# Seven weight tiles whose low halves are made by ScalarE and an adding transfer instead of VectorE

## The chip, the cores and the metric

The kernel runs on one core of one Trainium2 chip. A core has TensorE (matrix products), VectorE (DVE in the profile), ScalarE (ACT), GpSimd (POOL), SyncE (SP, which here only issues transfers) and 16 DMA engines that move data. The metric is the device time of one launch in microseconds, lower is better; the median of the runs is compared.

## The reference

One decoder layer on 256 tokens of width 1024, in float32. The input is normalised, multiplied by one wide weight matrix, and cut into the inputs of three token mixers, their gates and the merge logits:

```python
h = rmsnorm(x, g_in)
z = h @ w_in
(mq, mk, mv, mg, dq, dk, dv, dg, iq, ik, iw, xq, xg, glog) = jnp.split(z, offs, axis=-1)
ya = moba_attention(rope(mq), rope(mk), mv);  ya = (ya * silu(mg)) @ w_up_moba
yb = dsa_attention(rope(dq), rope(dk), dv, rope(iq), rope(ik), iw);  yb = (yb * silu(dg)) @ w_up_dsa
kv = rmsnorm(mem, g_mem) @ w_mem_kv
yc = cross_attention(xq, xk, xv);  yc = (yc * silu(xg)) @ w_up_cross
u = gates[:, :, 0] * ya + gates[:, :, 1] * yb + gates[:, :, 2] * yc
out = final_rmsnorm(x + u @ w_out)
```

With 256 tokens the first mixer is plain causal attention with 8 heads. The second lets each query see only the 64 keys with the highest score of an indexer; the kernel finds them in eight rounds of "take the eight largest". The third attends to 256 memory tokens with 4 heads.

## The kernel before

**Products in halves.** Each float32 operand is split into two numbers of TensorE's shorter float32 format (`F32R`): a high half, the operand rounded, and a low half, the operand minus its high half. Each product is then three matmuls: high by high, high by low, low by high. So each weight tile is needed three times over: as it is loaded (raw), as high half, as low half.

**Steps.** The weights are cut into tiles of 512 KB, 128 rows by 1024 columns of float32. `plan.steps` lists them in the order of use; one step is the matmuls of one tile. Steps 30 and 31 make the memory keys (first half), 32 and 33 the cross queries, 34 to 37 the values of the second mixer (`dv`), 38 and 39 the second half of the memory keys, 40 to 43 the memory values (`xv`), 44 onward the gates. Between the two halves of a step, and before it, stands other work that is due there: `at(step, fn)` puts it in `plan.side`. In the steps concerned here this is the attention of the first mixer (up to step 34), the indexer (27 to 42), the rotation of the second mixer's queries and keys (`qk_swap`, four transfers on SP each; `qk_rope` and `qk_halves`), and the first scores of the cross attention and of the second mixer from 41.5 on.

**Loads.** `load_weights(s)` (line 240) loads tile s from SP's queue into one of four raw buffers (`WRAW = 4`). It is written six steps ahead of its use, but a buffer must be free for it: all that read the old tile in it must be done.

**Splits.** `split_weights(s)` is written three steps ahead of use (`SPLIT_AHEAD = 3`). Line 253, on ScalarE, writes the high half `w..h`; line 255, on VectorE, writes the low half `w..l`:

```python
last_hi[0] = nc.scalar.copy(hi[:, ks, :], raw[:, ks, :]).ins
...
nc.vector.tensor_sub(lo[:, ks, :], raw[:, ks, :], hi[:, ks, :].bitcast(F32))
```

From step 4 on `part` is the whole tile, so there is one copy and one subtraction for each tile. High and low halves have five buffers each, so the split of tile s waits until TensorE is done with tile s - 5.

**Order.** TensorE's and GpSimd's instructions run in the order in which the program writes them (`manual_schedule`). For ScalarE, VectorE and SP a planner decides the order before the launch, from its own estimates of when each instruction could start. On each engine the instructions then run strictly one after the other, each waiting for its semaphores.

**GpSimd** has in the steps concerned only the scaling of the attention's probabilities (`self_scale`, line 622, two instructions for a head) and four small copies for the indexer (lines 445 and 446). It issues no transfer. The names in the profile: `mpr` are probabilities of the first mixer, `mtp` their transposes, `mph` and `mpl` the halves of these, `mya` and `myT` the attention's results, `msc` its scores, `mms` the masked scores, `lg` and `rl` the indexer's logits before and after the rectifier, `acc` their weighted sum, `iqt` and `ikt` transposes for the indexer, `dqT`, `dkT`, `dqsw`, `dksw` queries and keys of the second mixer and their swapped copies.

**Accumulators.** TensorE writes to eight banks: four for the steps' products, two for scores and logits (tag `sc`), one for transposes (`tp`), one for attention results (`y`). A bank that hasn't been read out holds up the next matmul that writes it.

Of the kernel before, what the change touches and what calls it, by code (L numbers as in the profile page):

```python
# [11 lines left out]
OP = mybir.AluOpType  # L12
# [69 lines left out]
LO_BEHIND = {29: "mpl0"}  # L82

MEM = (2, 7, 11, 15, 21.5)


def block_places(blocks, nk):
# [8 lines left out]
class Steps:  # L96
# [11 lines left out]
    def at(self, step, fn, *args):  # L108
        self.side[step].append((fn, args))
# [3 lines left out]
def hybrid_layer_kernel(  # L113
# [14 lines left out]
    nc = tc.nc  # L128
# [116 lines left out]
    def split_weights(s):  # L245
        raw = loaded.pop(s)
        shape = list(raw.shape)
        hi = ws.tile(shape, F32R, name=f"w{s}h", tag="whi")
        lo = ws.tile(shape, F32R, name=f"w{s}l", tag="wlo")
        part = 1 if s < HALVED + 2 else shape[1]  # L250
        for j in range(0, shape[1], part):
            ks = slice(j, j + part)
            last_hi[0] = nc.scalar.copy(hi[:, ks, :], raw[:, ks, :]).ins
            with tc.issue_after(marks[LO_BEHIND[s]]) if s in LO_BEHIND else nullcontext():
                nc.vector.tensor_sub(lo[:, ks, :], raw[:, ks, :], hi[:, ks, :].bitcast(F32))
        halves[s] = (hi, lo)
# [679 lines left out]

    for pair, s0 in enumerate(MEM[0:4]):
        at(s0, mem_load, pair)
# [4 lines left out]

    at(MEM[4], mem_stats)
    at(MEM[4] + 2, rstd_rows, m_rstd, mB, "mB")
    for hf in range(2):
# [43 lines left out]
    for s in range(-SPLIT_AHEAD, n):  # L990
        p, rest = divmod(s + SPLIT_AHEAD, 2)
        if p < 4 and not rest:
            first[p]()
        if s == 4:
            nc.sync.dma_start(cst, consts[:, 0:512])
            nc.sync.dma_start(tabT.rearrange("p t c -> p (t c)"), consts[:, 512:1024])
        for fn, args in plan.side.pop(s, []):
            fn(*args)
        if LOAD_AHEAD <= s + LOAD_AHEAD < n:
            load_weights(s + LOAD_AHEAD)  # L1000
        if s + SPLIT_AHEAD < n:
            split_weights(s + SPLIT_AHEAD)
            if s + SPLIT_AHEAD == 0:
                load_late()
        if s >= 0:
            w = halves.pop(s)
            plan.steps[s][1](w, 0)
            for fn, args in plan.side.pop(s + 0.5, []):
                fn(*args)
            plan.steps[s][1](w, 1)  # L1010
# [64 lines left out]
```

## Time and profile before

| what | before |
|---|---|
| median of 3 runs | 323.46 us (322.6 to 324.31) |
| profiled execution: span from the first to the last instruction | 321.2 us |
| median of the runs less that span | 2.3 us |
| TensorE busy | 313.0 us, 97% |
| VectorE busy | 252.1 us, 78% |
| ScalarE busy | 202.4 us, 63% |
| GpSimd busy | 42.1 us, 13% |
| transfers from GpSimd's queue | none |
| moved by all transfers | 59.45 MB, 185 GB/s on the mean |

The profile records one execution. For the profiled execution only its span is known, not a time of its own beside it; the time of a run holds also what lies before the first and after the last instruction. "Busy" is the time in which at least one instruction of an engine runs. TensorE's matmuls overlap, so gaps between them are read best from their starts. A row of the timeline has start, duration, engine, line, operation, output and inputs, and, in brackets, how long the engine had stood idle before it and who released it. A row of transfers has the queue that issued it, the count, the size, and the median time from issue to landing.

### The profile page before, as it was taken

What the parts mean: (1) busy time and instruction counts of PE and PEld (TensorE: products, weight loads), DVE (VectorE), ACT (ScalarE), POOL (GpSimd) and SP (SyncE); (2) the same over time, 40 slices, a digit from 0 to 9 for tenths busy, and PEclk for the clock granted to TensorE, in tenths of its full rate; (3) what the DMA queues carried; (4) which work ended last, traced back from release to release, by engine and by line L of the source; (5) the groups of instructions that cost most, each with busy time, mean ns of one, the idle gap of its engine ahead of it and who ended that gap; (6) DMA issues with size and microseconds to landing.
All of it is one profiled execution on the core that took longest, in us unless ns stands there. A gap on an engine that the chain in (4) does not pass through costs nothing.

```text
span 321.2 us, 6394 instructions
## 1 busy us (share of the span) xinstructions
PE 313.0 (97%) x2442; PEld 298.2 (93%) x2442; DVE 252.1 (78%) x458; ACT 202.4 (63%) x357; POOL 42.1 (13%) x58
## 2 busy tenths in 40 slices
PE   8999999999999999999999999999999999999992
PEld 7899999998999989889999999999999999998882
DVE  3579999999799999988866669999466866677533
ACT  5599665687877636477666688755454546653434
POOL 0001000017202000020200235411000111014011
PEclk9999999999999999999999999999999999999997
DMA  7999886965545346484444434488756666656003
GB/s 214 376 334 326 267 264 183 282 222 138 191 131 141 126 137 229 158 254 138 134 133 131 135 130 133 134 261 271 221 178 193 192 192 198 185 157 187 2 0 131
DMA packets 18367, 59.45 MB, mean 185 GB/s; under 512 B 2208, under 2 KB 2464, under 8 KB 18336
## 3 DMA queue, kind: packets, MB, share of 16 engines
q1 hardware_dynamic: 17760, 57.73, 57.3%
q10 hardware_dynamic: 576, 1.31, 1.1%
q8 instruction: 19, 0.31, 0.4%
q14 instruction: 12, 0.10, 0.1%
HBM read 55.89 MB, written 1.05 MB: 177 GB/s over the span
## 4 chain that ended last, share of the span: by engine, by line
PE 83%; ACT 5%; DVE 5%; DMA 3%; issue 2%; SPq 0%; ACTq 0%; DVEq 0%
DMA w3r<-w_in 2%; PE i_0ps L286 2%; PE i_1ps L286 2%; PE xv_0ps L286 2%; PE dv_0ps L286 2%; PE xv_1ps L286 2%; PE dv_1ps L286 2%; PE lg L486 1%; PE o_0ps L261 1%; PE o_0ps L262 1%; PE o_0ps L260 1%; DMA w0r<-w_in 1%; ACT mpr L612 1%; PE dya L648 1%; PE mv_1ps L286 1%
## 5 line engine op out<-in xcount | busy, mean ns | idle before, releaser
L753 POOL TENSOR_TENSOR u<-u,gt 128x512 f32<-128x512 f32 x7 | 9.9, 1413 | 76.7 <-DVE gt L750 76.7
L622 POOL TENSOR_SCALAR dpr<-dpr,dst 128x128 f32<-128x128 f32 (+1 forms) x16 | 6.6, 426 | 83.4 <-DVE dst L620 83.2
L622 POOL TENSOR_SCALAR mpr<-mpr,mst 128x128 f32<-128x128 f32 (+1 forms) x16 | 9.8, 628 | 56.0 <-DVE mst L620 56.0
L740 ACT ACTIVATE gt<-gt,x_first 128x256 f32<-128x256 f32 x24 | 10.9, 501 | 3.7 <-DVE gt L737 3.6
L612 ACT ACTIVATE dpr<-dms,dst 128x128 f32<-128x128 f32 (+1 forms) x16 | 7.1, 445 | 3.6 <-DVE dst L608 3.6
L612 ACT ACTIVATE mpr<-mms,mst 128x128 f32<-128x128 f32 (+1 forms) x16 | 7.1, 445 | 2.1 <-DVE mst L608 2.1
L794 ACT ACTIVATE junk<-xn 128x512 f32<-128x512 f32 (+1 forms) x5 | 2.7, 543 | 8.6 <-DVE xn L792 8.6
L670 ACT ACTIVATE xpr<-xsc,xst,xs_rstd 128x256 f32<-128x256 f32 x8 | 4.5, 560 | 4.1 <-DVE xst L666 4.1
L758 ACT CAST us<-u 128x512 fp32r<-128x512 f32 x4 | 2.5, 623 | 6.2 <-POOL u L753 4.9
L490 ACT ACTIVATE rl<-lg 128x384 f32<-128x384 f32 x8 | 3.9, 486 | 2.7 <-PE lg L486 1.6
L653 ACT COPY dyT<-dya 64x256 f32<-64x256 f32 x8 | 2.9, 368 | 4.2 <-PE dya L648 4.0
L493 DVE SCALAR_TENSOR_TENSOR acc<-rl,iw,acc 128x128 f32<-128x128 f32 (+1 forms) x14 | 5.4, 433 | 0.1
L974 PE MATMUL warm<-ones 128*128 128x128 f32 x18 | 4.2, 430 | 1.1 <-DVE eps_t L969 1.1
L486 PE MATMUL lg<-ikT,iqT 128*128 128x128 f32 (+1 forms) x32 | 5.1, 281 | 0.1
L608 DVE CUSTOM_DVE_ANT_0 mms<-msc,bias_c 128x128 f32<-128x128 f32 (+1 forms) x16 | 5.0, 348 | 0.0
L974 PEld LDWEIGHTS warm<-ones 128*128 128x128 f32 x18 | 3.9, 330 | 1.0 <-DVE eps_t L969 1.0
L635 DVE TENSOR_TENSOR dpl<-dtp,dph 128x384 fp32r<-128x384 f32 x8 | 4.4, 555 | 0.4
L654 DVE TENSOR_TENSOR dyT<-dyT,dya 64x256 f32<-64x256 f32 x8 | 3.3, 418 | 1.8 <-ACT dyT L653 1.7
L608 DVE CUSTOM_DVE_ANT_0 dms<-dsc,sel 128x128 f32<-128x128 f32 (+1 forms) x16 | 4.7, 353 | 0.0
L634 ACT CAST dph<-dtp 128x384 fp32r<-128x384 f32 x8 | 3.8, 479 | 1.4 <-PE dtp L633 1.3
L504 DVE MATCH_REPLACE8 wk<-m,wk 128x128 f32<-128x128 f32 (+1 forms) x14 | 4.7, 345 | 0.0
L792 DVE TENSOR_TENSOR xn<-o_0ps,xn 128x512 f32<-128x512 f32 x2 | 1.4, 692 | 4.2 <-PE o_0ps L262 4.2
(1296 smaller groups left out, 1544.3 us busy)
## 6 DMA issues: line engine op xcount, KB each, us to landing
x_rows<-x SPq DMA_DIRECT2D x2, 512.0 KB, 8.9
eT<-memT SPq DMA_DIRECT2D x4, 256.0 KB, 4.6
xn<-x SPq DMA_DIRECT2D x2, 512.0 KB, 4.8
w0r<-w_in SPq DMA_DIRECT2D x2, 256.0 KB, 3.3
w1r<-w_in SPq DMA_DIRECT2D x2, 256.0 KB, 4.3
xT<-xT SPq DMA_DIRECT2D x2, 256.0 KB, 6.6
w2r<-w_in SPq DMA_DIRECT2D x1, 512.0 KB, 6.7
w3r<-w_in ACTq DMA_DIRECT2D x1, 512.0 KB, 7.8
```

Of the source, the lines that this page charges most:

```text
L286: nc.tensor.matmul(accs[nm][t][:, :n], a[p](k, slice(t * P, (t + 1) * P)), w[q][:, half, :], start=k + i == 0, stop=k + i == nk + 1,)
L486: nc.tensor.matmul(lg[:, c : c + n], q[:, q0:q1], idx["k"][:, j, 0:n], start=j == 0, stop=j == 1)
L493: nc.vector.scalar_tensor_tensor(acc[:, c], rl[:, c], iw[:, t, g : g + 1], (bias_c if g == 0 else acc)[:, c], op0=OP.mult, op1=OP.add,)
L504: nc.vector.match_replace(out=wk[:, c], in_to_replace=m8[t], in_values=src[:, c], imm_value=TAKEN)
L608: nc.vector.tensor_tensor_reduce(out=ms[:, c], in0=sc[:, c], in1=bias()[:, c], op0=OP.add, op1=OP.min, scale=-(HD**-0.5), scalar=3e38, acc ...
L612: big["last_exp"] = nc.scalar.activation(pr[:, c], ms[:, c], AF.Exp, bias=st[:, t : t + 1], scale=-1.0, accum_out=st[:, 2 + t : 3 + t],)
L622: nc.gpsimd.tensor_scalar(pr[:, c], pr[:, c], st[:, 4 + t : 5 + t], 1.0, op0=OP.mult, op1=OP.mult)
L635: marks[f"{nm}pl{hd}"] = nc.vector.tensor_sub(pl, tp[:, 0 : 3 * P], ph.bitcast(F32)).ins
L670: big["last_exp"] = nc.scalar.activation(pr3[:, t, :], sc[:, t, :], AF.Exp, bias=st[:, t : t + 1], scale=xs_rstd[:, t : t + 1], accum_out= ...
L740: nc.scalar.activation(gt[:, f, :], gt[:, f, :], AF.Sigmoid, bias=x_first[:, j : j + 1])
L753: adder.tensor_tensor(u, u, gt, op=OP.add)
L974: nc.tensor.matmul(warm[:, 0:P], ones, ones, start=True, stop=True)
```

## The change

For seven tiles, every second one from step 31 to step 43, the low half is made in another way. ScalarE first rounds the raw tile to the high half as before. Then ScalarE multiplies the raw tile by -1 and writes it, rounded, into the low half's buffer: this is the high half negated. Then a transfer issued by GpSimd adds the raw tile to what stands in that buffer, which leaves raw minus high half. VectorE's subtraction is gone for these tiles; the other tiles are split as before.

```diff
+LO_ADDED = (31, 33, 35, 37, 39, 41, 43)
...
             last_hi[0] = nc.scalar.copy(hi[:, ks, :], raw[:, ks, :]).ins
+            if s in LO_ADDED:
+                nc.scalar.mul(lo[:, ks, :], raw[:, ks, :], -1.0)
+                nc.gpsimd.dma_start(lo[:, ks, :], raw[:, ks, :], accum_op=OP.add)
+                continue
             with tc.issue_after(marks[LO_BEHIND[s]]) if s in LO_BEHIND else nullcontext():
                 nc.vector.tensor_sub(lo[:, ks, :], raw[:, ks, :], hi[:, ks, :].bitcast(F32))
```

## The prediction

> **What bounds the kernel now.** I read the page's busy line and chain of waits first, then the table of windows, then the list of whom TensorE waited for, and last the timelines of each engine between 80 and 142 us, where tiles 31 to 43 are split.
>
> ```profile
> span 321.2 us, 6394 instructions
> PE 313.0 (97%) x2442; PEld 298.2 (93%) x2442; DVE 252.1 (78%) x458; ACT 202.4 (63%) x357; POOL 42.1 (13%) x58
> PE 83%; ACT 5%; DVE 5%; DMA 3%; issue 2%; SPq 0%; ACTq 0%; DVEq 0%
> ...
> 84.00:88.00 4.00, 3.79 (x36) 3.65 (x35) 3.94 (x7) 2.96 (x6) 0.00 (x0) 1.00 0.44 131
> 92.00:96.00 4.00, 3.88 (x36) 3.37 (x35) 3.94 (x15) 3.48 (x11) 0.00 (x0) 1.00 0.43 131
> 112.00:116.00 4.00, 4.00 (x19) 3.20 (x18) 3.94 (x13) 2.46 (x3) 0.00 (x0) 1.00 0.41 131
> ...
> 220.00:280.00 60.00, 60.00 (x517) 60.00 (x516) 40.04 (x38) 32.57 (x42) 5.17 (x4) 1.00 0.66 200
> ```
>
> TensorE is the bound: 97% busy, 83% of the chain, and the clock granted is full in these windows. After each colon pair the columns are length, then busy time of PE, PEld, DVE, ACT and POOL. VectorE (third busy figure) is nearly full from 84 to 116 us, 3.94 of 4.00, so it looks like a second bound; but a busy engine is worth something only where TensorE waits for it. In 112 to 116 us PE loses nothing, in 220 to 280 us neither. Where it does lose:
>
> ```profile
> PE iqt L459 <- DVE mst L608: 0.4, 1, 0.4
> PE ikt L463 <- DVE mpl L635: 0.2, 1, 0.2
> ...
> 79.47 0.28 PE L459 MATMUL iqt<-ident_r,iqs 128*128 128x128 f32 x1 [0.36 <-DVE mst L608]
> 85.23 0.36 PE L463 MATMUL ikt<-ident_r,iks 128*128 128x128 f32 x2 [0.21 <-DVE mpl L635]
> ...
> 92.25 0.33 PE L476 MATMUL msc<-mkhi,mqhi 64*128 64x128 f32 x2
> ...
> 92.93 0.28 PE L476 MATMUL msc<-mkhi,mqlo 64*128 64x256 f32 x2
> ...
> 94.42 0.28 PE L261 MATMUL dk1ps<-xlo,w29h 128*128 128x256 f32 x1
> 94.53 0.28 PE L262 MATMUL dk1ps<-xhi,w29l 128*128 128x256 f32 x1
> 94.93 0.73 PE L486 MATMUL lg<-ikT,iqT 128*128 128x128 f32 x4
> ```
>
> The 0.4 us wait for iqt ends at 79.47 us, before the first tile that the change touches is split (81.83, below). From tile 31 on, two places are left in the stretch of the change: 0.21 us before ikt, and 0.28 us before lg (0.40 from start to start where the matmuls before it come 0.11 to 0.12 apart). Together 0.49 us: with every removed VectorE instruction free, about 0.15% of the span is to be had there, since TensorE's order is written out and its matmuls follow each other without gaps elsewhere.
>
> **What is removed: seven subtractions on VectorE.** Line 255 takes 1.20 to 1.23 us for such a tile (two rows here), 8.5 us in all. What that is worth is read at the two places.
>
> ```profile
> 82.91 1.23 DVE L255 TENSOR_TENSOR w31l<-w31r,w31h 128x1024 fp32r<-128x1024 f32 x1 [1.41 <-ACT w31h L253]
> 84.62 0.56 DVE L635 TENSOR_TENSOR mpl<-mtp,mph 128x384 fp32r<-128x384 f32 x1
> ...
> 90.76 1.21 DVE L255 TENSOR_TENSOR w33l<-w33r,w33h 128x1024 fp32r<-128x1024 f32 x1
> ...
> 94.24 0.28 DVE L608 CUSTOM_DVE_ANT_0 mms<-msc,bias_c 128x128 f32<-128x128 f32 x1
> ```
>
> At lg: VectorE runs without a gap from w33l to mms, whose reading of the scores frees the bank that lg writes. Without w33l, mms could start once the scores are there, 92.93 + 0.28 = 93.2 us, over a microsecond earlier: the whole 0.28 us goes. At ikt: mpl follows w31l and a short addition; without w31l it is bounded by ScalarE's part, the next paragraph. The other five subtractions lie where PE loses nothing; taking them away is worth 0 there, hidden behind PE's own stream.
>
> **What is added on ScalarE: seven negations.** No row shows one with a scale of -1 on this shape; the nearest are the cast of the same tile (1.05 us) and the scaled copy below (two of 256 columns in 0.91 us, so up to 1.8 us for 1024). I take 1.05 us, the row of the same shape, 7.4 us in all.
>
> ```profile
> 81.83 1.05 ACT L253 CAST w31h<-w31r 128x1024 fp32r<-128x1024 f32 x1
> 82.90 0.36 ACT L653 COPY myT<-mya 64x256 f32<-64x256 f32 x1
> 83.29 0.48 ACT L634 CAST mph<-mtp 128x384 fp32r<-128x384 f32 x1
> ...
> 89.16 1.05 ACT L253 CAST w33h<-w33r 128x1024 fp32r<-128x1024 f32 x1 [0.76 <-PE dk1ps L261]
> 90.11 0.49 ACT L490 ACTIVATE rl<-lg 128x384 f32<-128x384 f32 x1
> 91.66 0.50 ACT L490 ACTIVATE rl<-lg 128x384 f32<-128x384 f32 x1 [1.06 <-PE lg L486]
> ...
> 108.61 1.05 ACT L253 CAST w37h<-w37r 128x1024 fp32r<-128x1024 f32 x1 [0.60 <-PE xq1ps L261]
> 120.43 1.05 ACT L253 CAST w41h<-w41r 128x1024 fp32r<-128x1024 f32 x1 [1.79 <-PE dv_1ps L286]
> ...
> 139.84 0.91 ACT L680 ACTIVATE xpr<-xpr,xst 128x256 f32<-128x256 f32 x2
> ```
>
> The scaled copy runs between exponentials with no table load, so I count none. Put right behind its cast, the negation of 31 holds back myT and mph by about 1.0 us: mph ends at 84.8 instead of 83.8, mpl can start there instead of at 84.62, and ikt is 0.2 us later than now. So this place gains nothing and loses 0.2. The negation of 33 falls into the gap of 1.06 us between the two rl; the first rl ends at 91.7 instead of 90.6, and the scores at 92.25 us that need its bank don't wait. From 108 us on ScalarE waits before almost every cast. Worth of both engines' edits together: 0.28 saved, 0.2 lost, about 0.1 us gained; the bounds are 0.49 gained and, without the gaps as cover, three negations before 104 us on the path, 3 x 1.05 = 3.2 us lost.
>
> **What is added on POOL: seven transfers.** They are issued from GpSimd's queue, in program order: 31 behind the scaling of head 5, 33 between head 6 and head 7, the rest behind head 7. Behind 33 waits only head 7's scaling, wanted by the transposes two steps later; behind 43 the next attention's scaling. The raw tile now stays occupied until its transfer has landed, and with it the load four tiles on, and everything behind that load on SP. Let X be the time from issue to landing. No transfer from GpSimd, and none that adds, is in this trace.
>
> ```profile
> q1 hardware_dynamic: 17760, 57.73, 57.3%
> x_rows<-x SPq DMA_DIRECT2D x2, 512.0 KB, 8.9
> w37r<-w_in SPq DMA_DIRECT2D x1, 512.0 KB, 3.7
> w41r<-w_kv SPq DMA_DIRECT2D x1, 512.0 KB, 3.5
> ...
> 96.81 1.82 POOL L622 TENSOR_SCALAR mpr<-mpr,mst 128x128 f32<-128x128 f32 x4 [14.64 <-DVE mst L620]
> 91.99 0.33 SPq L240 DMA_DIRECT2D w37r<-w_in  x1
> 97.31 1.15 SPq L530 DMA_DIRECT2D dksw<-dkT  x2
> 121.92 1.22 DVE L537 TENSOR_TENSOR dksw<-dksw,tabT 128x1024 f32<-128x1024 f32 x1
> ...
> 120.65 0.40 PE L286 MATMUL dv_0ps<-w37l,xhi 128*128 128x512 f32 x1
> 131.85 0.40 PE L286 MATMUL xv_0ps<-w41l,ehi 128*128 128x512 f32 x1
> ```
>
> A plain load of 512 KB lands in 3.5 to 3.7 us in this stretch. The addition reads its destination too; one tile's bytes cost 0.573 x 321.2 us x 0.524 MB / 57.73 MB = 1.7 us of all sixteen engines. For the issue on GpSimd I add 1 us, an estimate between the issue on SP (0.33) and the 1.82 us in which POOL does four instructions. X is then about 3.6 + 1.7 + 1 = 6.3 us; its bounds are a plain load, 3.5, and the slowest landing of this size, 8.9.
>
> The Trainium skill, "DMA: Bandwidth & Descriptors" (Anatomy of one DMA), fits a GpSimd transfer as 2.0 us plus its bytes at 436 GB/s, 3.2 us here. "Collectives: The Full Stack" (The bandwidth ceiling) says an addition in the DMA engine is slower because it reads two sources, not because it adds; with the bytes counted twice an estimate from the fit is 4.4 us. No row shows either; by them the margin worked out next would be wider and the sum the same.
>
> Which X hurts? The addition of 33 can't be issued before head 6 is scaled, 96.81 + 0.91 = 97.7 us, and lands at 97.7 + X. Only then does SP load w37, not at 91.99 but at 104.0; it lands 3.7 later, 107.7, in time for the cast at 108.61. (Behind that load wait dksw, issued at 97.31 now and read at 121.92, and the load of 38.) Cast and negation end at 110.7; the addition lands at 117.0, needed at 120.65. Load of w41: 117.0 + 3.5 = 120.5, cast 0.1 us late; cast, negation, addition: 120.5 + 2.1 + 6.3 = 128.9, needed at 131.85. Three microseconds to spare: the transfers are hidden and cost 0. For X over 7.2 each link slips and 41 lands at 109.1 + 3X, which is past 131.85 from **X = 7.6 us** on. The chain of 35, 39 and 43 is built in the same way.
>
> **Sum.** Span 321.2 - 0.1 = 321.1 us. The median of the runs, 323.46, is 2.3 us above the profiled span, which I carry over: 323.4 us.
>
> **Rivals.** (a) *The transfers are too slow*: X above 7.6. Place: w41's low half; price 3 us for each us of X beyond. At the slowest landing, 8.9, it lands at 135.8, 4.0 us late: 327.4 us, slower. For it: two reads, an issuer never measured here, weight loads on the same engines; against it: 6.3 by the rows. Chance 0.28. (b) *ScalarE becomes the limit before 104 us*: a negation ahead of evacuations that TensorE needs, three times 1.05: 326.6 us. For it: 3.48 of 4.00 busy in 92 to 96 us; against it: the gaps of 0.76 and 1.06 us in the rows. Chance 0.09. (c) *VectorE's relief counts in full*, because the planner puts the negations behind the evacuations: 0.49 us plus the 0.4 us at iqt, if its order changes that early: 322.6 us. Chance 0.14. (d) *VectorE isn't relieved*, the planner filling its place with waits for the same ScalarE outputs; that is 323.5 us, within the forecast. The forecast with (d) has 0.49.
>
> **How the numbers follow.** About 0.5% (1.6 us) can be told from no change. All of TensorE's losses that VectorE could have caused add up to less, so faster by more has 0.03, noise above all. Forecast, (d) and (c) less that give 0.60 for the same; (a) and (b) 0.37 for slower. The range runs from 322.3 (c and a little noise) to 327.4 (X at its upper bound): below lies some 0.05, above it 0.1. The forecast's own range is 322.8 to 324.2.
>
> **What would show it.** Right: the windows from 84 to 116 us show VectorE less busy, PE as busy as before; the gap before lg at 94.5 us gone; the transfers landing in 4 to 7.5 us; TensorE not waiting for any of w31l to w43l. Wrong: landings above 7.6 us, SP's loads of w37 and w41 issued past 105 and 119 us, and TensorE waiting for a transfer at w41l or w43l, which is (a); or TensorE waiting for mpl, rl or myT behind a negation, which is (b). Faster than 321.8 would mean that TensorE's stream has slack which these gaps don't show.

## The result, and the profile after

| what | before | after |
|---|---|---|
| median of the runs (four each) | 323.26 us (322.6 to 324.31) | 327.88 us (327.11 to 329.16) |
| profiled execution: span | 321.2 us | 325.5 us |
| VectorE busy | 252.1 us | 245.5 us |
| ScalarE busy | 202.4 us | 208.8 us |
| GpSimd busy | 42.1 us | 49.4 us |

The changed kernel is slower: ratio 1.0148, 95% interval 1.0115 to 1.0181, about 4.6 us. The busy line of the page after, its new transfer queue and its chain of waits:

```profile
PE 314.2 (97%) x2442; PEld 298.5 (92%) x2442; DVE 245.5 (75%) x451; ACT 208.8 (64%) x364; POOL 49.4 (15%) x65
...
q0 software_dynamic: 1008, 3.67, 6.0%
...
PE 75%; DMA 8%; ACT 7%; DVE 5%; issue 4%; ACTq 0%; DVEq 0%; POOLq 0%; SPq 0%
DMA w41l<-w41r 3%; DMA w37l<-w37r 2%; PE mv_0ps L292 2%; PE i_0ps L292 2%; PE mv_1ps L292 2%; PE i_1ps L292 2%; DMA w45r<-w_in 2%; PE warm L980 1%; DMA w41r<-w_kv 1%; PE o_0ps L267 1%; PE lg L492 1%; PE o_0ps L268 1%; PE o_0ps L266 1%; ACT mpr L618 1%; PE dya L654 1%
```

VectorE has seven instructions less and is 6.6 us less busy, ScalarE seven more and 6.4 us busier. TensorE's share of the chain fell from 83% to 75%, that of transfers rose from 3% to 8%, and the last line names them: the additions of 41 and 37, and the loads of 45 and 41.

**Where the time went** is read from TensorE's timeline. The first matmul of steps 31, 43, 44 and 52, before and then after:

```profile
99.99 0.28 PE L260 MATMUL xk_0ps<-ehi,w31h 128*128 128x256 f32 x1
137.69 0.40 PE L286 MATMUL xv_0ps<-w43h,ehi 128*128 128x512 f32 x1
141.92 0.37 PE L260 MATMUL mg0ps<-xhi,w44h 128*128 128x256 f32 x1
174.00 0.38 PE L260 MATMUL xg0ps<-xhi,w52h 128*128 128x256 f32 x1
```

```profile
99.44 0.28 PE L266 MATMUL xk_0ps<-ehi,w31h 128*128 128x256 f32 x1
137.69 0.40 PE L292 MATMUL xv_0ps<-w43h,ehi 128*128 128x512 f32 x1
141.43 0.32 PE L482 MATMUL dsc<-dkhi,dqhi 64*128 64x128 f32 x1 [1.93 <-ACT xpr L676]
144.16 0.36 PE L266 MATMUL mg0ps<-xhi,w44h 128*128 128x256 f32 x1
177.93 0.38 PE L266 MATMUL xg0ps<-xhi,w52h 128*128 128x256 f32 x1
```

From 31 to 43 it took 37.70 us before and 38.25 after (0.55 lost), from 43 to 44 4.23 and 6.47 (2.24 lost), from 44 to 52 32.08 and 33.77 (1.69 lost): 74.01 and 78.49 us in all, 4.48 lost. From 52 to the first matmul of step 95 it is 126.94 and 126.93 us, and from 27 to 31 19.41 and 19.23: nothing lost after, 0.2 gained ahead. So the loss sits between 131 and 157 us, at the last converted tiles and behind them. The list of whom TensorE waited for, after:

```profile
PE dsc L482 <- ACT xpr L676: 1.9, 1, 1.9
...
PE ikt L469 <- DVE mpl L641: 0.4, 1, 0.4
...
PE xv_0ps L292 <- DMA w41l<-w41r: 0.3, 1, 0.3
```

Only 0.3 us stands against a transfer. The largest new wait, 1.9 us, names the exponentials of the cross attention (`xpr`), which have no converted tile among their inputs (`dsc`, the second mixer's first scores, needs a bank that the cross scores fill until the exponentials have read them). SyncE's queue leads on; its waits (total, times, longest), then the list of transfers (count, size, us from issue to landing):

```profile
SPq L242 <- DMA w41l<-w41r: 9.2, 1, 9.2
SPq L242 <- DMA w37l<-w37r: 8.1, 1, 8.1
```

```profile
w31l<-w31r POOLq DMA_DIRECT2D x1, 512.0 KB, 4.5
w33l<-w33r POOLq DMA_DIRECT2D x1, 512.0 KB, 6.3
w35l<-w35r POOLq DMA_DIRECT2D x1, 512.0 KB, 6.7
w37l<-w37r POOLq DMA_DIRECT2D x1, 512.0 KB, 7.1
w39l<-w39r POOLq DMA_DIRECT2D x1, 512.0 KB, 4.8
w41l<-w41r POOLq DMA_DIRECT2D x1, 512.0 KB, 8.5
w43l<-w43r POOLq DMA_DIRECT2D x1, 512.0 KB, 6.1
w45r<-w_in SPq DMA_DIRECT2D x1, 512.0 KB, 5.1
```

Loads wait for the additions to let go of their raw buffers. The longest of these waits, 9.6 us for the addition of 31, holds the load of 35 and does no harm: steps 32 to 40 take as long as before. The rows of GpSimd, SyncE, ScalarE and VectorE show how this reaches `xpr`:

```profile
110.38 0.86 POOL L258 DMA_DIRECT2D w37l<-w37r  x1 [7.75 <-ACT w37l L257]
117.50 0.33 SPq L242 DMA_DIRECT2D w41r<-w_kv  x1
121.81 1.06 ACT L257 ACTIVATE w41l<-w41r 128x1024 fp32r<-128x1024 f32 x1 [0.17 <-DMA w41r<-w_kv]
123.17 0.85 POOL L258 DMA_DIRECT2D w41l<-w41r  x1 [7.19 <-ACT w41l L257]
131.76 0.33 SPq L242 DMA_DIRECT2D w45r<-w_in  x1
...
136.96 1.05 ACT L255 CAST w45h<-w45r 128x1024 fp32r<-128x1024 f32 x1 [6.05 <-DMA w45r<-w_in]
138.04 1.22 DVE L261 TENSOR_TENSOR w45l<-w45r,w45h 128x1024 fp32r<-128x1024 f32 x1 [6.04 <-ACT w45h L255]
139.19 0.68 DVE L671 TENSOR_REDUCE xst<-xsc 128x2 f32<-128x512 f32 x1
140.18 0.56 ACT L676 ACTIVATE xpr<-xsc,xst,xs_rstd 128x256 f32<-128x256 f32 x1 [2.17 <-DVE xst L672]
```

The addition of 37 lands at 110.38 + 7.1 = 117.5 us, and the load of 41 starts at 117.50. The addition of 41 lands at 123.17 + 8.5 = 131.7, and the load of 45 starts at 131.76. It lands at 131.76 + 5.1 = 136.9, and there ScalarE, which had stood idle for 6.05 us, casts 45. VectorE, idle for 6.04 us, subtracts 45, and only then reduces the cross scores (`xst`), for which the exponentials wait, for which TensorE waits. Tile 45 itself isn't needed before step 45, behind the whole of step 44. What it costs is its place: on ScalarE its cast stands ahead of `xpr`, on VectorE its subtraction stands ahead of `xst`. The same rows before, under the landing time of `w45r`:

```profile
w45r<-w_in SPq DMA_DIRECT2D x1, 512.0 KB, 4.5
...
125.63 0.33 SPq L240 DMA_DIRECT2D w45r<-w_in  x1
132.58 1.05 ACT L253 CAST w45h<-w45r 128x1024 fp32r<-128x1024 f32 x1
136.24 0.69 DVE L665 TENSOR_REDUCE xst<-xsc 128x2 f32<-128x512 f32 x1
137.37 1.22 DVE L255 TENSOR_TENSOR w45l<-w45r,w45h 128x1024 fp32r<-128x1024 f32 x1
137.56 0.56 ACT L670 ACTIVATE xpr<-xsc,xst,xs_rstd 128x256 f32<-128x256 f32 x1 [1.37 <-DVE xst L666]
```

There the load of 45 was issued 6.1 us earlier, and the reduction ran ahead of the subtraction of 45: the edit also changed VectorE's planned order, which puts more behind the late load (experiment 1 shows this order without a late load). The table of windows shows the size of the hole, 131 to 142 us, before and then after (length, then busy time of PE, PEld, DVE, ACT, POOL):

```profile
131.00:142.00 11.00, 11.00 (x62) 8.81 (x60) 11.00 (x28) 6.48 (x13) 0.00 (x0) 1.00 0.71 205
```

```profile
131.00:142.00 11.00, 8.79 (x46) 6.67 (x47) 3.15 (x6) 2.87 (x6) 0.00 (x0) 1.00 0.80 263
```

VectorE fell from 11.00 busy of 11.00 to 3.15, ScalarE from 6.48 to 2.87, at an unchanged clock. What they would have done here they do later, while steps 44 to 46 run, and there TensorE loses the remaining 1.7 us, most of it in four places where the next matmul starts 0.28 to 0.44 us later than usual (before the products with `xpl`, for one).

### The profile page after: what moved, and what is told of

Read it like the earlier page. It is cut to its first block, busy times and chain, and to the rows that moved or that the text cites. A ratio compares the mean times of both kernels' runs of the same rounds, so it can differ in the third digit from the quotient of the medians.

```text
span 325.5 us, 6408 instructions
## 1 busy us (share of the span) xinstructions
PE 314.2 (97%) x2442; PEld 298.5 (92%) x2442; DVE 245.5 (75%) x451; ACT 208.8 (64%) x364; POOL 49.4 (15%) x65
## 3 DMA queue, kind: packets, MB, share of 16 engines
HBM read 55.89 MB, written 1.05 MB: 175 GB/s over the span
## 4 chain that ended last, share of the span: by engine, by line
PE 75%; DMA 8%; ACT 7%; DVE 5%; issue 4%; ACTq 0%; DVEq 0%; POOLq 0%; SPq 0%
DMA w41l<-w41r 3%; DMA w37l<-w37r 2%; PE mv_0ps L292 2%; PE i_0ps L292 2%; PE mv_1ps L292 2%; PE i_1ps L292 2%; DMA w45r<-w_in 2%; PE warm L980 1%; DMA w41r<-w_kv 1%; PE o_0ps L267 1%; PE lg L492 1%; PE o_0ps L268 1%; PE o_0ps L266 1%; ACT mpr L618 1%; PE dya L654 1%
## 5 line engine op out<-in xcount | busy, mean ns | idle before, releaser
L628 POOL TENSOR_SCALAR mpr<-mpr,mst 128x128 f32<-128x128 f32 (+1 forms) x16 | 11.1, 787 | 52.9 <-DVE mst L626 52.9
L261 DVE TENSOR_TENSOR w45l<-w45r,w45h 128x1024 fp32r<-128x1024 f32 x1 | 1.2, 1224 | 6.0 <-ACT w45h L255 6.0
L919 POOL COPY bias_c<-cst 128x128 f32<-128x128 f32 x1 | 1.2, 1231 | 25.2 <-DMA cst<-consts 25.2
L804 POOL TENSOR_TENSOR xn<-xn,gf 128x512 f32<-128x512 f32 x2 | 2.6, 1294 | 15.9 <-ACT junk L800 15.9
L255 ACT CAST w45h<-w45r 128x1024 fp32r<-128x1024 f32 x1 | 1.0, 1048 | 6.0 <-DMA w45r<-w_in 6.0
L482 PE MATMUL dsc<-dkhi,dqhi 64*128 64x128 f32 (+1 forms) x16 | 3.0, 326 | 1.9 <-ACT xpr L676 1.9
```

The costliest lines, as they stand in the source:

```text
L628: nc.gpsimd.tensor_scalar(pr[:, c], pr[:, c], st[:, 4 + t : 5 + t], 1.0, op0=OP.mult, op1=OP.mult)
```

## The experiments

Four theories stood against each other. **Theory 1**: the chain of held raw buffers (37, 41, 45) and then the order on ScalarE and VectorE behind the cast of 45. **Theory 2**: the seven negations on ScalarE, the prediction's rival (b). **Theory 3**: the bytes of the additions slow all transfers. **Theory 4**: every converted tile costs a share, 4.5 us / 7 = 0.6 us. Because the first loads of the kernel land at different times from one profile to the next (with four raw buffers, step 31 starts between 99.0 and 101.6 us), the stretches are compared beside the totals, and the issue of the load of 45 is given from the start of step 31 (in after 131.76 - 99.44 = 32.3 us):

| kernel | 31 to 43 | 43 to 44 | 44 to 52 | 31 to 52, us | lost, us | load of 45, us behind the start of 31 | ratio to before (95%) |
|---|---|---|---|---|---|---|---|
| before | 37.70 | 4.23 | 32.08 | 74.01 | 0 | 25.6 | 1 |
| after | 38.25 | 6.47 | 33.77 | 78.49 | 4.48 | 32.3 | 1.0148 (1.0115 to 1.0181) |
| negate_only | 37.70 | 4.23 | 32.09 | 74.02 | 0.01 | 24.1 | 0.9991 (0.9978 to 1.0004) |
| five_raw | 37.93 | 4.23 | 32.08 | 74.24 | 0.23 | 22.3 | 1.0149 (1.0107 to 1.0191) |
| before_five_raw | 37.70 | 4.22 | 32.09 | 74.01 | 0 | 22.0 | 1.0129 (1.0098 to 1.016) |
| cast45_behind | 37.95 | 4.24 | 32.37 | 74.56 | 0.55 | 32.0 | 1.0054 (1.0035 to 1.0074) |
| without_41 | 37.70 | 4.23 | 32.08 | 74.01 | 0 | 24.9 | 1.0009 (0.9991 to 1.0027) |
| only_41 | 37.70 | 4.22 | 32.91 | 74.83 | 0.82 | 28.2 | 1.0026 (1.0012 to 1.0039) |
| without_37 | 37.70 | 4.23 | 32.24 | 74.17 | 0.16 | 26.0 | 1.0012 (0.9996 to 1.0029) |
| only_31_33 | 37.86 | 4.24 | 32.10 | 74.20 | 0.19 | 26.1 | 0.9996 (0.9983 to 1.001) |
| plain_copy | 37.71 | 4.82 | 33.76 | 76.29 | 2.28 | 30.4 | 1.0073 (1.0058 to 1.0088) |
| before_cast45 | 37.70 | 4.23 | 33.85 | 75.78 | 1.77 | 25.7 | 1.0053 (1.0028 to 1.0077) |

**1. The negations alone** (negate_only). The transfers are left out, so the seven low halves hold the negated high half.

```diff
                 nc.scalar.mul(lo[:, ks, :], raw[:, ks, :], -1.0)
-                nc.gpsimd.dma_start(lo[:, ks, :], raw[:, ks, :], accum_op=OP.add)
                 continue
```

> The seven transfers are left out; VectorE's subtractions stay out and ScalarE's negations stay in, so the low halves of these tiles are the negated high halves and the products miss their low parts. Theory 1 (a raw buffer is held until its transfer has landed, so the load of tile 45 comes late and ScalarE and VectorE stand behind its cast): without transfers nothing is held, about 323.0 us, and TensorE's wait before the second mixer's first scores (1.9 us) is gone. Theory 2 (ScalarE's seven extra instructions, 7.4 us, push its evacuations back): the time stays at 327 to 328 us. Theory 3 (the transfers' bytes slow the other loads): like theory 1, about 323.0.

Measured: 323.19 us against 323.35 us of before. ScalarE has its seven negations and VectorE lacks its seven subtractions, and the time is that of before: theory 2 falls, and so does any hope in VectorE's relief, since this kernel gives the edit without the price of its transfers. The load of 45 is no longer late: it is issued 24.1 us behind the start of step 31 (25.6 in before). VectorE has the order of after here:

```profile
133.00 1.23 DVE L260 TENSOR_TENSOR w45l<-w45r,w45h 128x1024 fp32r<-128x1024 f32 x1 [0.17 <-ACT w45h L255]
134.14 0.68 DVE L670 TENSOR_REDUCE xst<-xsc 128x2 f32<-128x512 f32 x1
```

So the new order by itself costs nothing; it takes a late tile 45 to make it harmful.

**2. and 3. A fifth raw buffer**, with the change (five_raw) and without it (before_five_raw). A scratch tile (tag `t2`, in two places) gets one buffer in place of two, for the room: the fifth raw buffer takes 4 KB in each row, and 2 KB of them come from there.

```diff
-WRAW = 4
+WRAW = 5
...
-        t2 = work.tile([P, 512], F32, name=f"{nm}t2", tag="t2")
+        t2 = work.tile([P, 512], F32, name=f"{nm}t2", tag="t2", bufs=1)
...
-        sg = work.tile([P, 2, S], F32, name=f"{nm}sg{hf}", tag="t2")
+        sg = work.tile([P, 2, S], F32, name=f"{nm}sg{hf}", tag="t2", bufs=1)
```

> The changed kernel with five raw buffers instead of four; the 2 KB a row that this takes come from one scratch tile of the rotation and the gates (tag t2), which has one buffer instead of two. Theory 1: the load of tile 45 no longer waits for tile 41's transfer, 323 to 324.5 us. Theory 2: 327 to 328 us, since ScalarE does the same. Theory 3: 327 to 328 us, since the same bytes move in the same stretch.

> The kernel before with the same five raw buffers and the same single t2 buffer, as the measure for five_raw. All theories: 323.3 us within 1 us; any gain or loss here belongs to the buffers, not to the change.

Measured: 327.57 us and 327.68 us. By its total the first looks as if buffers had nothing to do with it. But the fifth buffer, with the scratch tile's single one, costs 4.3 us by itself, so the second expectation was missed, and so was that of theory 1 for the first, whose total can't be read without it: with five buffers the change makes next to no difference (ratios 1.0149 and 1.0129 to the same kernel). The stretch from 31 to 52 is 74.24 us, 4.25 of the 4.48 us back. Step 31 starts 4.6 us later in before_five_raw than in before. Of this 2.95 us are there by the first matmul of step 3, as its transfers and TensorE's waits show (the rest comes between steps 23 and 31, where the single scratch buffer may have a part; the two weren't run apart):

```profile
w3r<-w_in ACTq DMA_DIRECT2D x1, 512.0 KB, 10.6
...
PE mq_0ps L260 <- ACT w3h L253: 2.1, 1, 2.1
```

The load of tile 4 no longer waits for a buffer; it starts at 4.48 us in place of 6.99, ahead of that of tile 3 (6.20), which lands in 10.6 us (7.8 before). TensorE then waits for tile 3.

**4. The cast of 45 behind the exponentials** (cast45_behind): the edit ties only ScalarE's order, and all additions stay. The planner then also puts the reduction of the cross scores ahead of 45's subtraction on VectorE (135.57 and 139.40 us).

```diff
-            last_hi[0] = nc.scalar.copy(hi[:, ks, :], raw[:, ks, :]).ins
+            with tc.issue_after(big["last_exp"].ins) if s == 45 else nullcontext():
+                last_hi[0] = nc.scalar.copy(hi[:, ks, :], raw[:, ks, :]).ins
```

> The changed kernel, with ScalarE's cast of tile 45 tied behind the exponentials of the first cross-attention head, so that a late load of 45 can't hold these up. Theory 1 in its form that the harm is done by what stands behind the cast on ScalarE and VectorE: 1.9 to 2.5 us come back, 325.3 to 326.0 us, and the wait before the second mixer's first scores is gone. If instead tile 45 itself comes too late for TensorE: 327.9 us or more, with TensorE waiting for tile 45. Theory 2: 327 to 328 us.

```profile
133.57 0.33 SPq L242 DMA_DIRECT2D w45r<-w_in  x1
136.58 0.56 ACT L677 ACTIVATE xpr<-xsc,xst,xs_rstd 128x256 f32<-128x256 f32 x1 [3.45 <-DVE xst L673]
...
138.31 1.05 ACT L256 CAST w45h<-w45r 128x1024 fp32r<-128x1024 f32 x1 [0.54 <-DMA w45r<-w_in]
```

Measured: 324.98 us. The load of 45 is as late as in after (32.0 us behind the start of step 31), but `xpr` runs ahead of the cast, the wait at `dsc` is gone, and the stretch is 74.56 us: 3.93 of 4.48 us back with every transfer in place, more than the 1.9 to 2.5 us expected. So most of the loss isn't the late tile but the work queued behind it. The total stays 0.54% above before, some 1.7 us, of which the stretch has 0.55 (0.25 of it in step 41, whose low half is late here too). In its profile the rest lies ahead of step 31, which starts 1.6 us later than in before; the first loads took longer to land (`w1r` 5.9 us against 4.3). Why this kernel starts more slowly is open.

**5. and 6. Tile 41 left out, and tile 41 alone** (without_41, only_41).

```diff
-LO_ADDED = (31, 33, 35, 37, 39, 41, 43)
+LO_ADDED = (31, 33, 35, 37, 39, 43)
```

```diff
+LO_ADDED = (41,)
```

> Tile 41 is split as before; the other six stay changed. Theory 1, the chain of held buffers (33 holds 37, 37 holds 41, 41 holds 45): 41's buffer is free after VectorE's subtraction, some 2.5 us behind its cast, so the load of 45 is issued near 125 us, as before, and nothing waits: 323 to 324 us. Theory 4, a share for each tile (4.6 us over seven): 327.2 us.

> Only tile 41 is changed. Theory 1: 41's own load is not late now, so its cast starts near 120.4 us, its transfer is issued near 122.5 and lands by 128 to 129 us, with the load of 45 in by 133 us: up to 1 us late against the cast's place, 323.3 to 324.3 us. A fault of tile 41 alone (its transfer's 8.5 us): 326 to 328 us. Theory 4: 323.9 us.

Measured: 323.71 us without 41, 324.20 us with 41 alone (before 323.05). With six of seven tiles converted nothing measurable is lost, and the stretch is 74.01 us. That is against theory 4, which wants 6/7 of the loss, and against theory 3, since the six additions still take 5.3% of the DMA engines' span (seven took 6.0%), and the load of 45 took even longer to land (6.0 us, 5.1 in after). Tile 41 alone loses 0.8 us of the 4.5, nearly all of it in step 46. Its load isn't late there, since no addition of 37 holds it up, and its own addition lands in 6.8 us. The load of 45 is issued at 123.90 us without 41 and at 128.93 us with 41 alone.

Where the order on ScalarE and VectorE is the planner's own, the issue of 45 orders the kernels (table): up to 26 us behind the start of step 31 it costs next to nothing, at 28.2 us 0.8, at 30.4 us 2.3, at 32.3 us 4.5 us. Of the losses of 0.2 us in the table, that of five_raw lies in step 41, whose low half comes late there too (its addition takes 8.5 us); those of without_37 (step 46) and only_31_33 (step 40) are not explained.

**7. The link before** (without_37: 37 left out, 41 converted).

```diff
-LO_ADDED = (31, 33, 35, 37, 39, 41, 43)
+LO_ADDED = (31, 33, 35, 39, 41, 43)
```

> Tile 37 is split as before, the other six stay changed, so the chain of held buffers is cut one link earlier than in the run without 41. Theory 1: the load of 41 is issued near 112 us instead of 117.5, its transfer lands near 128 to 129, and what is left is what the run with 41 alone showed, 323.8 to 324.6 us; TensorE doesn't wait for w41l. Theory 4, a share for each tile: 327.2 us.

```profile
126.41 0.33 SPq L242 DMA_DIRECT2D w45r<-w_in  x1
133.58 1.05 ACT L255 CAST w45h<-w45r 128x1024 fp32r<-128x1024 f32 x1 [0.94 <-DMA w45r<-w_in]
```

Measured: 323.58 us against 323.16. The load of 41 starts at 112.45 us, the addition of 41 lands in 4.7 us in place of 8.5, 45 is loaded at 126.41, and the stretch is 74.17 us. The addition of 41 is done at 126.4 us, earlier than the 128 to 129 expected, so less is left than in only_41. Either link taken out, 37 or 41, ends the loss: it is the chain of both, as theory 1 has it.

**8. The first two tiles** (only_31_33).

```diff
-LO_ADDED = (31, 33, 35, 37, 39, 41, 43)
+LO_ADDED = (31, 33)
```

> Only tiles 31 and 33 are changed, the two whose subtractions stood ahead of TensorE's waits. Theory 1: 37's load is up to 5 us later and still in time, 323.0 us, at best 0.3 us under the kernel before by the wait before lg. Theory 4: 324.6 us.

Measured: 323.05 us, as before (323.05). From 27 to 31 TensorE takes 19.21 us in place of 19.41: the 0.2 us at `lg` is there and too small to be told in the total.

**9. A plain copy in place of the addition** (plain_copy): same instructions, orders and bytes written, but nothing is added to what stands in the destination. The low halves hold the whole tile.

```diff
-                nc.gpsimd.dma_start(lo[:, ks, :], raw[:, ks, :], accum_op=OP.add)
+                nc.gpsimd.dma_start(lo[:, ks, :], raw[:, ks, :])
```

> The seven transfers copy the raw tile into the low half's buffer instead of adding it, so the low halves hold the whole tile and the products are not the reference's; all engines' orders are those of the changed kernel. If the second read of the addition makes the landings long: they fall from 4.5 to 8.5 us to 3.5 to 6 us, the load of 45 is issued 3 us earlier, and the time falls to 324 to 326 us. If it is the issue on GpSimd and the crowd of loads released together: landings and time stay, 327 to 328 us.

```profile
w31l<-w31r POOLq DMA_DIRECT2D x1, 512.0 KB, 3.0
w37l<-w37r POOLq DMA_DIRECT2D x1, 512.0 KB, 2.9
w41l<-w41r POOLq DMA_DIRECT2D x1, 512.0 KB, 6.9
```

Measured: 325.86 us, inside the 324 to 326 of the first expectation. Tile 31 lands in 3.0 us (4.5 with the addition), 37 in 2.9 (7.1), 41 in 6.9 (8.5). The load of 45 starts 30.4 us behind the start of step 31, 1.9 us earlier than in after (3 expected), and the loss in the stretch is 2.28 us, half of 4.48. The addition, with its second read and its longer issue (0.85 us on GpSimd for 41, 0.53 for the copy), is therefore about half the price. The other half is that a transfer holds the raw buffer at all, and that it runs beside loads: even the plain copy of 41 takes 6.9 us.

**10. The tie of experiment 4 in the kernel before** (before_cast45), with the same edit as there.

> The kernel before with only the tie of tile 45's cast behind the exponentials, as the measure for cast45_behind, which was 1.6 us over the kernel before. If the tie itself costs something: 324 us or more. If what was left there belongs to the transfers and to the loads of the first microseconds: 323.0 to 323.5 us, and the stretch from step 31 to step 52 takes 74.0 us as before.

Measured: 324.56 us against 323.16; the expectation was missed. Here the late cast costs 1.8 us in steps 44 and 45, where TensorE waits for VectorE:

```profile
PE xsc L261 <- DVE dst L609: 0.9, 1, 0.9
```

The subtractions of 45, 46 and 47, held up by the late cast, stand on VectorE ahead of the reading of the second mixer's scores, which starts at 143.64 us in place of 140.87. So the tie isn't a repair that could be kept: in an undisturbed kernel the planner's own order is better. For experiment 4 this means that its 3.9 us came back in spite of what the tie itself may cost. No kernel of these is faster than before beyond its interval: negate_only, which doesn't pay for the transfers, bounds the gain of the idea at 0.22% (0.9978).

## Why the prediction was wrong, point by point

It forecast 323.4 us and no change; the time is 327.88, above its range.

- **What VectorE's relief is worth: right.** The prediction read a reachable gain of 0.49 us and a net of 0.1. Stretch 27 to 31 gained 0.18 us, the gap at `lg` is gone (0.12 us from start to start, 0.40 before), and the wait at `ikt` went from 0.2 to 0.4 us, the loss foreseen there. That VectorE at 3.94 of 4.00 busy isn't a bound was shown by negate_only.
- **The negations: right.** They take 1.05 to 1.07 us, and the price of ScalarE's burden, rival (b), is nothing. VectorE was relieved (29.05 us busy from 84 to 116 us, 31.29 before), so rival (d) falls too; rival (c) wanted 0.8 us below the forecast, and negate_only, which has the relief without the transfers, is 0.16 us below before.
- **The time of a transfer X: right at its mean by luck, wrong as one number.** GpSimd's issue takes 0.85 to 1.03 us (1 estimated), the addition of 31 took 4.5 - 3.0 = 1.5 us longer than the copy, issue included (1.7 estimated for the second read alone). The mean of the seven is 6.3 us, the number taken, but they run from 4.5 to 8.5, and the longest is the last link of the chain. The agreement is luck, for the addition of 31 took 4.5 us, with the DMA engines 0.59 busy until it landed; the other six ran with them 0.85 to 1.01 busy, and a price for that was no term of the sum. The base of the sum, 3.5 to 3.7 us for a plain load, came from tiles 37 and 41 alone: the loads of 31 to 45 took 3.4 to 5.3 us in before. The Trainium skill, "DMA: Bandwidth & Descriptors" (Anatomy of one DMA), gives by its fit an estimate of 3.2 us for a GpSimd transfer of this size: the plain copies of 31 and 37 agree (3.0 and 2.9 us), that of 41, which runs beside the loads released with it, doesn't (6.9).
- **The chain up to 41: nearly right.** Predicted and measured: addition of 37 landed 117.0 and 117.5 us, load of 41 landed 120.5 and 121.7, addition of 41 issued after 122.6 and at 123.17, landed 128.9 and 131.7. Where the link of 33 was seen wrongly (37 was loaded at 99.19 us, not 104.0; 38 took 33's buffer), it made no difference, because the addition of 37 waited for its negation anyway (row of 110.38 above). Of the three microseconds to spare nothing was left: w41's low half was 0.55 us late.
- **The step that failed** is the sentence "Three microseconds to spare: the transfers are hidden and cost 0". It compared the landing of 41 with the need of TensorE for 41, and ended there. But two wait for this landing: TensorE, and the load that takes over the raw buffer. The prediction had named this link for 33, 37 and 41 ("with it the load four tiles on, and everything behind that load on SP") and didn't apply it once more, to 45. Nor did it ask what is queued behind the cast of 45 on ScalarE and behind its subtraction on VectorE. By its own numbers (landing at 128.9) the load of 45 would have come 3.3 us later than the 125.63 us of before, and with the landing time of before (`w45r`, 4.5 us) tile 45 would be in at 128.9 + 4.5 = 133.4, past the 132.58 us at which ScalarE cast it. In after the addition of 41 landed at 131.7 and tile 45 at 136.9. The rows of before held this warning. A load at 128.9 us is 28.9 behind the start of step 31, and at such a lateness the runs lost 0.8 us (only_41, 28.2) to 2.3 us (plain_copy, 30.4).
- **Rival (a) was right on its cause and wrong on its place and price.** It had landings above 7.6 us and 327.4 us in the worst case, close to the time measured, but by a stall of 4.0 us at w41's low half. That stall is 0.55 us; 3.9 us arise one link on. Its threshold for X was too high for the same reason: X is 6.8 us for 41 in only_41 and costs 0.8 us already. Of the marks set down for it, the loads past 105 and 119 us didn't appear (99.19 and 117.50), and "TensorE waiting for a transfer at w41l" would have shown it with 0.3 us only and missed the mechanism.

## What to carry to other kernels

When a change lengthens the time for which a buffer is held, follow the buffer and not only the data: to the load that takes it over, to the consumer of that load, and to everything that stands behind this consumer on its in-order engines, until a link has slack that the rows show. A tile that its own matmuls don't wait for can still stop two engines, here for 6 us, because its cast stands in the queue ahead of work that is due. And an idle-looking wait that names an uninvolved producer (`xpr`) is best followed back through what that engine last waited for.

## What the runs showed of the hardware that was not expected

- An adding transfer of 512 KB took 4.5 to 8.5 us, a plain copy in its place 2.9 to 6.9 us. The longest addition, that of 41, ran beside loads that stood closer together than before: 41, behind the addition of 37, 42 behind it on SP, 43, behind the addition of 39, and 44 were issued within 4.2 us (10.0 before), the last three 1.5 to 5.2 us ahead of it. The table of windows has the DMA engines at 0.99 of their time there, where before it was 0.55 (last but one figure; before, then after):

```profile
118.00:131.00 13.00, 13.00 (x82) 11.54 (x81) 13.00 (x26) 6.84 (x8) 0.00 (x0) 1.00 0.55 189
```

```profile
118.00:131.00 13.00, 13.00 (x81) 11.59 (x80) 12.93 (x31) 8.82 (x11) 1.83 (x2) 1.00 0.99 273
```

  So a held buffer can bunch the loads that it delays. That the bunching made the addition of 41 slow is not shown: it fits without_37, where 41 took 4.7 us, but not only_41, where no addition holds up a load and 41 took 6.8 us, with the DMA engines about as busy until it landed (0.92 and 0.91). A converted tile cost 6.0 / 7 = 0.86% of the DMA engines' span with the addition and 0.5% with the plain copy.
- With one load buffer more, and one scratch buffer less, the kernel was 1.3% slower (before_five_raw): the load of tile 4 started 2.5 us earlier, ahead of that of tile 3, which is needed first and landed in 10.6 us in place of 7.8. In five_raw it took 10.5 us, in the kernels with four buffers 6.7 to 8.7.
